# A hybrid attention and DeltaNet block: two operands of a block solve turned by VectorE's 32x32 transposes instead of trips through DRAM

## The chip, the cores and the metric

The kernel runs on one core of a Trainium2 chip. The metric is the device time of one execution in microseconds, lower is better. Engines are named as in the profile: PE (TensorE) multiplies matrices, DVE (VectorE) and ACT (ScalarE) work elementwise, POOL (GpSimd) here sets constants and issues transfers, SP (SyncE) only issues transfers. Each engine takes its instructions in the order in which they stand in its own stream.

## The reference, cut to what matters

One decoder block on 1024 tokens of width 1024: an RMS norm, one wide input projection, two mixers, their gates, an output projection, a residual, a final norm. Mixer A is a dilated window attention. Mixer B, where the change lies, is a gated DeltaNet in chunks of 64 tokens: for each of 8 heads and 16 chunks a unit lower triangular 64x64 matrix must be inverted.

```
k_beta = kc * bc[..., None]
a = jnp.einsum('bhnid,bhnjd->bhnij', k_beta, kc) * decay_strict
t_inv = lax.linalg.triangular_solve(eye + a, jnp.broadcast_to(eye, a.shape),
                                    left_side=True, lower=True, unit_diagonal=True)
u = t_inv @ (vc * bc[..., None])
w = t_inv @ (k_beta * jnp.exp(G)[..., None])
```

All arithmetic is in float32 as far as the output can tell; the kernel splits operands of the large products in two float16 parts and adds three products.

## The kernel before, in words

**Order of the work.** TensorE's order is written out by hand: `Feed` hands out steps of the large projections (three 128x512 products with 512 columns each, about 0.65 us a step), and the small mixers' products are put between them by `feed.tick(n)`. For the other engines a scheduler sets the order when the kernel is built, from priorities and its own idea of times. What stands in an engine's stream is then taken strictly in that order.

**The inverse.** The 8 heads are handled in two halves, `hb` 0 and 1, 64 matrices each. A matrix is cut in 32x32 blocks. `keys_side` (line 1275) makes from the keys the two scalars of each row, `brk` (beta over the key's norm) and `rk` (one over the norm), packs them in `pack`, lets TensorE form the products of keys (`pairs`), multiplies by the decays and leaves the result, transposed, in `MT[hb]`. The diagonal blocks go to DRAM (`m_d`) and come back in `As` with one 32x32 block in each partition. The scalars take the same way: transposed by TensorE (line 1294), copied by ACT (line 1296), stored to `sc_d`, loaded as `bsc` with a block in each partition.

`solve` (line 1305) multiplies `As` by the two scalars (two products on DVE), and in 31 steps of two DVE instructions each (`stmp<-As,X`, then `X<-X,stmp`) builds the inverse of all 128 diagonal blocks in `X`. It scales `X` and writes minus its transpose to `T1`, **which takes the buffer of `As`**: the pool has one buffer with that tag. `X` and `T1` are stored to `u_d` and `t_d`. Four loads bring the blocks of `X` back into `MT[hb]` (called `U` there), two loads bring `T1p`, the operand of the merge, in a layout with a block row in each partition. `T1p` shares the tag and the one buffer with `kd`, a product of the keys that `spill_keys` (line 1214) stores.

The whole solve is recorded with a lowered priority, so the scheduler puts its steps between other DVE work.

`merge` (line 1339) makes the block below the diagonal. `left(g)`: 32 small products of `T1p` and `U` into a bank `ps_S` (L1350), which DVE evicts as `Y`, scaled by `brk` from `pack`. `right(g)`: 32 products of `Y` and `U` into `ps_G` (L1365), copied into `U` by ACT. In TensorE's order stand `left(0)`, five feed steps, `left(1)` interleaved with `right(0)`, five feed steps, `right(1)`. `state_parts` (line 1384) then multiplies `U` by values (`rvt`, L1413) and keys (`kbt`, L1417), evicted as `uw`.

**What runs around it.** While the solves run on DVE, TensorE projects units of the DeltaNet (`gdn`) and gates. Each half of a `gdn` unit (24 products, one of three `ps_mm` banks) is copied by ACT into `xc` and `ca` (two buffers each); DVE adds three shifted products (`ca`, line 83, three in a chain); ACT applies SiLU. The second values unit, projected from 637 to 659 us, is transposed on TensorE by four groups of L1440 into `ps_O`, a tag with **one** bank, evicted by DVE as `rv`. For every unit of weights ACT writes `whi` and DVE `wlo`, two halves each. The queue of SP holds nearly all of these loads and stores, in order: a transfer that waits holds up those behind it.

Of the kernel before, what the change touches and what calls it, by code (L numbers as in the profile page):

```python
# [10 lines left out]
F32 = mybir.dt.float32  # L11
# [3 lines left out]
ALU = mybir.AluOpType  # L15
# [62 lines left out]
def hybrid_block(ctx: ExitStack, tc: tile.TileContext, A):  # L78
    nc = tc.nc
    V, SC, PE, GP = nc.vector, nc.scalar, nc.tensor, nc.gpsimd  # L80
# [4 lines left out]
    def TT(out, in0, in1, op, eng=None):  # L85
        (eng or V).tensor_tensor(out, in0, in1, op)  # L86
# [5 lines left out]
    def bank(tag, bufs):  # L92
        return ps.tile([128, 512], F32, name=f"ps_{tag}", tag=tag, bufs=bufs)
# [26 lines left out]
    def part(n):  # L120
        off[0] += n
        return cons[:, off[0] - n:off[0]]

    ident = part(128)
# [371 lines left out]
    with tc.manual_schedule(engines={nc.vector.engine, nc.scalar.engine}):  # L496
        wq, wk = w_first
        q, k = qk
# [63 lines left out]
        q = [bank("mm", 3), bank("O", 1)]  # L562
# [580 lines left out]
    p2_ = pctx.enter_context(tc.tile_pool(name="gpre2", bufs=1))  # L1143
# [25 lines left out]
    def rnorm(dst, ssum, post):  # L1169

        SC.activation(ssum, ssum, AF.Sqrt, bias=epsc)
        V.reciprocal(dst, ssum)
        if post != 1.0:
            V.tensor_scalar(dst, dst, post, None, op0=ALU.mult)

    def heads_h2(x):
        return x.rearrange("p t (q e) -> p t e q", e=2)
# [34 lines left out]
    def spill_keys(hb):  # L1212

        hs = slice(4 * hb, 4 * hb + 4)
        for g in range(2):
            ts = slice(4 * g, 4 * g + 4)
            k = key_rows(hb, g)
            kd = p2_.tile([128, 4, 4, 64], F32, name="kd", tag="T1p", bufs=1)
            TT(kd, k, bc(eGl[:, ts, hs], 64), ALU.mult)
            nc.sync.dma_start(out=kd_d[ts, :, hs].rearrange("t p h c -> p t h c"), in_=kd)  # L1220
            TT(k, k, bc(bgk[:, ts, hs], 64), ALU.mult)
            nc.sync.dma_start(out=kb_d[hb][:, ts], in_=k)

    def sumsq(hb, src, dst, take=None):

        for t0 in range(0, 8, 2):
            p = bank("S", 2)
            for t in (0, 1):
                for c in range(2):
                    o = (2 * t + c) * 128  # L1230
                    PE.transpose(p[:, o:o + 128],
                                 src[2 * hb + c][:, 2 * (t0 + t):2 * (t0 + t) + 2].rearrange("p c i -> p (c i)"), ident)
            if take:
                take(hb, t0, p)
            with tc.high_priority():
                SC.activation(p, p, AF.Square)
                V.tensor_reduce(dst[:, t0:t0 + 2], p.rearrange("p (t h c) -> p t h c", t=2, c=64), AX.X, ALU.add)
            feed.tick(2)
# [36 lines left out]
    def keys_side(hb):  # L1275
        hsl = slice(4 * hb, 4 * hb + 4)
        sumsq(hb, kT, kss, keep_keys)
        rnorm(rk[:, :, hsl], kss, 1.0)
        TT(brk[:, :, hsl], rk[:, :, hsl], beta[:, :, hsl], ALU.mult)
        TT(bgk[:, :, hsl], brk[:, :, hsl], eG[:, :, hsl], ALU.mult)  # L1280
        pack = p2_.tile([128, 2, 8, 4], F32, name="pack", tag="pack", bufs=2)
        packs.append(pack[:, 0].rearrange("p t h -> p (t h)"))
        for i, x in enumerate((brk, rk)):
            V.tensor_copy(pack[:, i].rearrange("p t (e q) -> p t e q", e=2), heads_h2(x[:, :, hsl]))
        pairs(hb, kT, MT[hb])
        spill_keys(hb)
        m_d = tc.dram_tile([4, 32, 32, 32], F32, name=f"m_d{hb}")
        for kb in range(4):
            b = kb % 2
            nc.sync.dma_start(out=m_d[kb].rearrange("n j i -> j n i"),  # L1290
                              in_=MT[hb][32 * kb:32 * kb + 32].rearrange("p t e q i -> p (t e q) i")[:, :, 32 * b:32 * b + 32])
        feed.tick(4)
        pp = bank("G", 2)
        PE.transpose(pp[0:64, 0:128], pack.rearrange("p a t h -> p (a t h)"), ident)
        packT = p2_.tile([64, 128], F32, name="packT", tag="packT", bufs=1)
        SC.copy(packT, pp[0:64, 0:128])
        sc_d = tc.dram_tile([2, 4, 32, 32], F32, name=f"sc_d{hb}")
        for i in range(2):
            nc.sync.dma_start(out=sc_d[i].rearrange("k n i -> n k i"),
                              in_=packT[32 * i:32 * i + 32].rearrange("p (k i) -> p k i", i=32))  # L1300
        bsc = p2_.tile([128, 2, 32], F32, name="bsc", tag="bsc", bufs=2)
        nc.sync.dma_start(out=bsc, in_=sc_d.rearrange("a k n i -> (k n) a i"))
        return m_d, bsc

    def solve(hb, m_d, bsc):

        As = p2_.tile([128, 32, 32], F32, name="As", tag="As", bufs=1)
        nc.sync.dma_start(out=As.rearrange("p j i -> p (j i)"), in_=m_d.rearrange("k n j i -> (k n) (j i)"))
        TT(As, As, bsc[:, 0, None, :].to_broadcast([128, 32, 32]), ALU.mult)
        TT(As, As, bsc[:, 1, :, None].to_broadcast([128, 32, 32]), ALU.mult)  # L1310
        X = p2_.tile([128, 32, 32], F32, name="X", tag="X", bufs=1)
        GP.memset(X, 0.0)
        GP.memset(X.rearrange("p a b -> p (a b)")[:, ::33], 1.0)
        for k in range(31):
            n = 31 - k
            tmp = p2_.tile([128, 256], F32, name="stmp", tag="stmp", bufs=1)
            tv = tmp[:, :(k + 1) * n].rearrange("p (a b) -> p a b", b=n)
            TT(tv, As[:, k:k + 1, k + 1:].to_broadcast([128, k + 1, n]),
               X[:, :k + 1, k:k + 1].to_broadcast([128, k + 1, n]), ALU.mult)
            TT(X[:, :k + 1, k + 1:], X[:, :k + 1, k + 1:], tv, ALU.subtract)  # L1320
        TT(X, X, bsc[:, 1, None, :].to_broadcast([128, 32, 32]), ALU.mult)
        T1 = p2_.tile([128, 32, 32], F32, name="T1", tag="As", bufs=1)
        V.tensor_scalar(T1, X.rearrange("p j i -> p i j"), -1.0, None, op0=ALU.mult)
        u_d = tc.dram_tile([4, 32, 32, 32], F32, name=f"u_d{hb}")
        t_d = tc.dram_tile([4, 32, 32, 32], F32, name=f"t_d{hb}")
        nc.sync.dma_start(out=u_d.rearrange("k n j i -> (k n) (j i)"), in_=X.rearrange("p j i -> p (j i)"))
        nc.sync.dma_start(out=t_d.rearrange("k n j i -> (k n) (j i)"), in_=T1.rearrange("p j i -> p (j i)"))
        U = MT[hb]
        T1p = p2_.tile([128, 8, 4, 32], F32, name="T1p", tag="T1p", bufs=1)
        for kb in range(4):  # L1330
            b = kb % 2
            if b == 0:
                nc.sync.dma_start(out=T1p[32 * kb:32 * kb + 32].rearrange("p t h j -> p (t h) j"),
                                  in_=t_d[kb].rearrange("n i j -> i n j"))
            nc.sync.dma_start(out=U[32 * kb:32 * kb + 32].rearrange("p t e q i -> p (t e q) i")[:, :, 32 * b:32 * b + 32],
                              in_=u_d[kb].rearrange("n j i -> j n i"))
        return T1p
# [118 lines left out]
    for hb in range(2):  # L1456
        conv_unit(hb, 0, lambda c, hb=hb: qT[2 * hb + c],
                  lambda c, q, hb=hb: nc.scalar.dma_start(out=q_d[2 * hb + c], in_=q))
    gate_unit(5, gate_spill)
    side, solved, packs = [], [], []  # L1460
    for hb in range(2):
        decay(hb)
        side.append(keys_side(hb))
        with tc.high_priority(offset=-SOLVE_LATER):
            solved.append(solve(hb, *side[hb]))
# [206 lines left out]
    for t in range(8):  # L1672
# [21 lines left out]
        for c2 in range(2):  # L1694
            ch = 2 * t + c2
            ov = ob[:, t, 4 * c2:4 * c2 + 4]
            if ch:

                pwq = [bank("S", 2), bank("S", 2)]
                for i in range(2):  # L1700
                    for q in range(2):
                        for e, hb in ((0, 0), (1, 1), (0, 1), (1, 0)):
                            b, c, o = c2 ^ hb, 2 * hb + q, (2 * i + q) * 64
# [44 lines left out]
    for h0 in (0, 2):  # L1748
        for hf in range(2):
# [6 lines left out]
            for hb in range(2):  # L1756
# [8 lines left out]
                n = osp["b", ct]  # L1765
# [19 lines left out]
    for n in range(7):  # L1785
        wo7[n] = []
        for i, l in enumerate("hl"):
            if n == 5:
                t = [late[0].tile([128, 512], F32, name=f"wo5{l}{b}", tag=("gst", "oa")[i], bufs=2).bitcast(F16)
                     .rearrange("p (k n) -> p k n", n=512) for b in range(2)]  # L1790
                wo7[n].append(lambda k, t=t: t[k // 2][:, k % 2])
                continue
            if n == 6:
                t = late[1].tile([128, 2, S], F16, name=f"wo6{l}", tag="oTb", bufs=6)
                t = t.rearrange("p a b -> p (a b)").rearrange("p (k n) -> p k n", n=512)
            else:
                t = fp2.tile([128, 4, 512], F16, name=f"wo{n}{l}")
# [6 lines left out]
                            bufs=1 if n < 4 else 6).rearrange("p l (k i) -> p l k i", i=256) for n in range(7)])  # L1804
# [33 lines left out]
    for pair in range(4):  # L1838
        hf, ps_ = pair // 2, slice(pair % 2 * 128, pair % 2 * 128 + 128)
        rows_ = [Tokens(2 * pair + i) for i in range(2)]  # L1840
        x, q, y = [bank(*b) for b in ((("G", 2), ("G", 2), ("mm", 3)), (("mm", 3),) * 3)[pair % 2]]
# [160 lines left out]
```

## Time and profile before

| | |
|---|---|
| Runs, us | 1072.23, 1076.85, 1076.34; median 1076.34 |
| Profiled execution, us | 1075.46 |
| Its span, first to last instruction, us | 1073.7 |
| Granted TensorE clock, mean | 0.997 |
| Busy in the span: PE, DVE, ACT | 1048.7, 864.4, 559.6 us |
| First solve on DVE | 604.87 to 645.8 us |
| Second solve on DVE | 670.38 to 712.5 us |
| First merge on TensorE, from its first product to the start of `right(1)` | 666.68 to 676.59 us |
| Second merge, the same | 730.27 to 743.30 us |

How to read it: a row of the timeline has the start and the length in us, the engine, the line (a helper's line where a helper records the instruction: L86 is every `tensor_tensor` and L83 every `scalar_tensor_tensor`), the operation, the tile written and the tiles read, shapes, and a count where rows are merged. In square brackets stands the idle time of the engine before the row and what ended it. A row of stretches has for each engine the busy time in the stretch, the granted clock (1.00 is full speed), the busy share of the DMA engines and GB/s. Matmuls overlap: 128x512 products last 0.38 us each and start 0.216 us apart at full clock.

### The profile page before, as it was taken

What the parts mean: (1) busy time and instruction counts of PE and PEld (TensorE: products, weight loads), DVE (VectorE), ACT (ScalarE), POOL (GpSimd) and SP (SyncE); (2) the same over time, 40 slices, a digit from 0 to 9 for tenths busy, and PEclk for the clock granted to TensorE, in tenths of its full rate; (3) what the DMA queues carried; (4) which work ended last, traced back from release to release, by engine and by line L of the source; (5) the groups of instructions that cost most, each with busy time, mean ns of one, the idle gap of its engine ahead of it and who ended that gap; (6) DMA issues with size and microseconds to landing.
All of it is one profiled execution on the core that took longest, in us unless ns stands there. A gap on an engine that the chain in (4) does not pass through costs nothing.

```text
span 1073.7 us, 23669 instructions
## 1 busy us (share of the span) xinstructions
PE 1048.7 (98%) x9398; PEld 639.1 (60%) x9398; DVE 864.4 (81%) x1982; ACT 559.6 (52%) x1272; POOL 56.1 (5%) x107
## 2 busy tenths in 40 slices
PE   7999999999999999999999999999999999999997
PEld 5995585775956855765645544555545555444443
DVE  6897997869878788979966897986588778899834
ACT  6455766566666656547645623244454345443522
POOL 0000000000000000000000000111200000000000
PEclk9999999999999999999999999999999999999999
DMA  8144531632615432641234357785685433763132
GB/s 278 61 131 106 140 105 50 173 95 80 191 67 149 109 105 61 178 120 50 76 123 159 91 130 196 245 242 158 200 267 166 147 98 121 274 225 109 61 117 79
DMA packets 99488, 148.47 MB, mean 138 GB/s; under 512 B 31136, under 2 KB 64416, under 8 KB 98224
## 3 DMA queue, kind: packets, MB, share of 16 engines
q1 hardware_dynamic: 68976, 84.60, 27.4%
q0 software_dynamic: 12320, 44.11, 13.2%
q10 hardware_dynamic: 18080, 18.23, 4.9%
q8 instruction: 74, 1.21, 0.5%
q14 instruction: 38, 0.31, 0.1%
HBM read 91.13 MB, written 36.90 MB: 119 GB/s over the span
## 4 chain that ended last, share of the span: by engine, by line
PE 61%; DVE 27%; ACT 5%; issue 3%; DMA 2%; SPq 1%; ACTq 0%; DVEq 0%
PE ps_mm L183 15%; PE ps_mm L184 14%; PE ps_mm L185 14%; DVE ca L83 4%; DVE wlo L83 2%; DVE X L86 2%; DVE stmp L86 2%; DVE sm L799 2%; PE ps_S L184 2%; PE ps_S L185 2%; PE ps_S L183 2%; DVE tl L86 1%; PE ps_G L813 1%; DVE rt L86 1%; ACT sm L803 1%
## 5 line engine op out<-in xcount | busy, mean ns | idle before, releaser
L185 PE MATMUL ps_mm<-h_hi,wlo 128*128 128x512 f16 (+1 forms) x552 | 208.3, 377 | 0.0
L183 PE MATMUL ps_mm<-h_hi,whi 128*128 128x512 f16 (+1 forms) x492 | 185.6, 377 | 0.0
L184 PE MATMUL ps_mm<-h_lo,whi 128*128 128x512 f16 (+1 forms) x492 | 185.5, 377 | 0.0
L185 PEld LDWEIGHTS <-wlo 128*128 128x128 f16 x788 | 77.2, 98 | 86.5 <-issue 0.6
L183 PEld LDWEIGHTS <-whi 128*128 128x128 f16 x848 | 83.3, 98 | 69.2 <-issue 0.9
L184 PEld LDWEIGHTS <-whi 128*128 128x128 f16 x848 | 83.2, 98 | 68.0 <-issue 1.2
L183 PE MATMUL ps_mm<-whi,h_hi 128*128 128x256 f16 x384 | 105.1, 274 | 0.0
L185 PE MATMUL ps_mm<-whi,h_lo 128*128 128x256 f16 x384 | 104.7, 273 | 0.0
L184 PE MATMUL ps_mm<-wlo,h_hi 128*128 128x256 f16 x384 | 104.7, 273 | 0.0
L803 ACT ACTIVATE sm<-sm,osb 128x128 f32<-128x128 f32 (+1 forms) x160 | 69.5, 435 | 65.0 <-DVE osb L799 60.5
L86 DVE TENSOR_TENSOR tl<-ps_G,th 128x256 f16<-128x256 f32 (+1 forms) x96 | 52.0, 542 | 21.9 <-ACT th L818 21.4
L83 DVE SCALAR_TENSOR_TENSOR wlo<-wstage,whi 128x1024 f16<-128x1024 f32 x50 | 61.0, 1220 | 3.4 <-ACT whi L166 3.2
L799 DVE CUSTOM_DVE_ANT_0 sm<-ps_S,amask 128x128 f32<-128x128 f32 (+1 forms) x192 | 59.4, 348 | 5.2 <-PE ps_S L792 5.2
L83 DVE SCALAR_TENSOR_TENSOR ca<-xc,cw,ca 128x512 f32<-128x512 f32 x72 | 53.9, 748 | 5.3 <-ACT ca L1010 4.6
L166 ACT ACTIVATE whi<-wstage 128x1024 f16<-128x1024 f32 x49 | 51.4, 1051 | 1.7 <-ACT gst L948 0.8
L83 DVE SCALAR_TENSOR_TENSOR whi<-wstage,whi 128x512 f16<-128x512 f32 x60 | 40.9, 689 | 13.6 <-ACT whi L330 13.0
L813 PE MATMUL ps_G<-cons,sm 128*128 128x128 f32 x280 | 47.9, 275 | 3.1 <-ACT sm L803 1.3
L813 PEld LDWEIGHTS ps_G<-cons,sm 128*128 128x128 f32 x280 | 35.5, 141 | 19.3 <-ACT sm L803 4.9
L184 PEld LDWEIGHTS <-h_hi 128*128 128x128 f16 x384 | 45.8, 119 | 1.6
L330 ACT ACTIVATE whi<-wstage 128x512 f16<-128x512 f32 x60 | 37.1, 627 | 18.4 <-DVE wstage L329 13.3
L183 PE MATMUL ps_mm<-h_hi,wlo 128*128 128x512 f16 x120 | 45.6, 380 | 1.0 <-DVE rx L83 1.0
L183 PEld LDWEIGHTS <-h_hi 128*128 128x128 f16 x384 | 45.6, 119 | 1.5
(445 smaller groups left out, 2593.3 us busy)
## 6 DMA issues: line engine op xcount, KB each, us to landing
wstage<-in_w POOLq DMA_DIRECT2D x68, 512.0 KB, 4.6
og<-osb ACTq DMA_DIRECT2D x32, 132.0 KB, 2.1
og<-og SPq DMA_DIRECT2D x32, 132.0 KB, 2.2
gspb<-gst ACTq DMA_DIRECT2D x16, 256.0 KB, 2.5
sga<-gspa SPq DMA_DIRECT2D x8, 512.0 KB, 6.4
wstage<-in_w_up POOLq DMA_DIRECT2D x8, 512.0 KB, 4.7
wos<-in_w_out SPq DMA_DIRECT2D x8, 512.0 KB, 5.3
sgb<-gspb SPq DMA_DIRECT2D x8, 512.0 KB, 5.1
```

Of the source, the lines that this page charges most:

```text
L83: (eng or V).scalar_tensor_tensor(out, in0, scalar, in1, op0=op0, op1=op1)
L86: (eng or V).tensor_tensor(out, in0, in1, op)
L166: in_turn(SC.activation(hi[:, 4 * c:4 * c + 4], st, AF.Copy, scale=W_SCALE))
L183: PE.matmul(out, lhsT=wh(k), rhs=mh(k), start=first and i == 0, stop=False, skip_group_check=True)
L184: PE.matmul(out, lhsT=wh(k), rhs=ml(k), start=False, stop=False, skip_group_check=True)
L185: last_pe[0] = PE.matmul(out, lhsT=wl(k), rhs=mh(k), start=False, stop=last and i == len(ks) - 1, skip_group_check=True).ins.name
L330: in_turn(SC.activation(t[:, b, 0], self.part[name], AF.Copy, scale=W_SCALE))
L799: V.tensor_tensor_reduce(P[:, u, :128 * nk], psc[:, u * 256:u * 256 + 128 * nk], mask, -cexp, -NEG, ALU.add, ALU.min, accum_out=osb[:, 256 ...
L803: SC.activation(P[:, u, :128 * nk], P[:, u, :128 * nk], AF.Exp, bias=osb[:, 256 + hd:257 + hd], scale=-1.0, accum_out=osb[:, 260 + hd:261 ...
L813: PE.transpose(pt[:, c:c + 128], P[:, u, i * 128:i * 128 + 128], ident)
```

## The change

Four edits, all in `keys_side` and `solve`.

1. `pack` is filled by multiplications, `brk` times -1 and `rk` times 1, instead of copies, and `bsc` is made from `pack` by one VectorE transpose in 32x32 blocks. The transpose on TensorE, the copy on ACT, `sc_d` and its four stores and two loads (both halves) go.
2. As the scalar now has the minus sign, the solve adds where it subtracted.
3. `T1p` is written from `X` by one VectorE transpose in 32x32 blocks, straight into the merge's layout. `T1`, `t_d`, its store and the two loads of `T1p` in each half go. So nothing takes `As`'s buffer at the end of a solve any more. The merge's sign sits in `brk`, by which `Y` is scaled.
4. The four loads of `U` come in the order 1, 3, 0, 2.

```diff
         for i, x in enumerate((brk, rk)):
-            V.tensor_copy(pack[:, i].rearrange("p t (e q) -> p t e q", e=2), heads_h2(x[:, :, hsl]))
+            V.tensor_scalar(pack[:, i].rearrange("p t (e q) -> p t e q", e=2), heads_h2(x[:, :, hsl]),
+                            (-1.0, 1.0)[i], None, op0=ALU.mult)
+        bsc = p2_.tile([128, 2, 32], F32, name="bsc", tag="bsc", bufs=2)
+        V.transpose(bsc.rearrange("p a i -> p (a i)"), pack.rearrange("p a t h -> p (a t h)"))
...
-        pp = bank("G", 2)
-        PE.transpose(pp[0:64, 0:128], pack.rearrange("p a t h -> p (a t h)"), ident)
-        packT = p2_.tile([64, 128], F32, name="packT", tag="packT", bufs=1)
-        SC.copy(packT, pp[0:64, 0:128])
-        sc_d = tc.dram_tile([2, 4, 32, 32], F32, name=f"sc_d{hb}")
-        for i in range(2):
-            nc.sync.dma_start(out=sc_d[i].rearrange("k n i -> n k i"),
-                              in_=packT[32 * i:32 * i + 32].rearrange("p (k i) -> p k i", i=32))
-        bsc = p2_.tile([128, 2, 32], F32, name="bsc", tag="bsc", bufs=2)
-        nc.sync.dma_start(out=bsc, in_=sc_d.rearrange("a k n i -> (k n) a i"))
...
-            TT(X[:, :k + 1, k + 1:], X[:, :k + 1, k + 1:], tv, ALU.subtract)
+            TT(X[:, :k + 1, k + 1:], X[:, :k + 1, k + 1:], tv, ALU.add)
         TT(X, X, bsc[:, 1, None, :].to_broadcast([128, 32, 32]), ALU.mult)
-        T1 = p2_.tile([128, 32, 32], F32, name="T1", tag="As", bufs=1)
-        V.tensor_scalar(T1, X.rearrange("p j i -> p i j"), -1.0, None, op0=ALU.mult)
+        T1p = p2_.tile([128, 8, 4, 32], F32, name="T1p", tag="T1p", bufs=1)
+        V.transpose(T1p.rearrange("p t h j -> p j (t h)"), X)
...
-        t_d = tc.dram_tile([4, 32, 32, 32], F32, name=f"t_d{hb}")
...
-        nc.sync.dma_start(out=t_d.rearrange("k n j i -> (k n) (j i)"), in_=T1.rearrange("p j i -> p (j i)"))
...
-        T1p = p2_.tile([128, 8, 4, 32], F32, name="T1p", tag="T1p", bufs=1)
-        for kb in range(4):
+        for kb in (1, 3, 0, 2):
...
-            if b == 0:
-                nc.sync.dma_start(out=T1p[32 * kb:32 * kb + 32].rearrange("p t h j -> p (t h) j"),
-                                  in_=t_d[kb].rearrange("n i j -> i n j"))
```

The change also moves instructions that it doesn't touch, since the scheduler orders anew. TensorE's order is the same but for the two transposes. Rows below are of the two built programs; the lines of the changed kernel are its own, 13 lower behind the edits.

SP, from the last stores ahead of the end of the first solve. Before, the second load of `As` stands behind all traffic of the first solve's result:

```order
L1326 DMA u_d_8342<-X 128x1024
L1327 DMA t_d_8343<-T_8340 128x1024
L1335 DMA MT_7877<-u_d_8342 32x32x32
L1333 DMA T1p<-t_d_8343 32x32x32
L1335 DMA MT_7877<-u_d_8342 32x32x32
L1333 DMA T1p<-t_d_8343 32x32x32
L1335 DMA MT_7877<-u_d_8342 32x32x32
L1446 DMA rv_d<-rv 128x4x128
L1335 DMA MT_7877<-u_d_8342 32x32x32
L1446 DMA rv_d<-rv 128x4x128
L1392 DMA rvt<-rv_d 128x4x256
L1308 DMA As<-m_d_8711 128x1024
```

SP in the changed kernel, the same place:

```order
L1433 DMA rv_d<-rv 128x4x128 x2
L1301 DMA As<-m_d_8701 128x1024
L1318 DMA u_d_8335<-X 128x1024
L1322 DMA MT_7877<-u_d_8335 32x32x32 x4
L1433 DMA rv_d<-rv 128x4x128
L1379 DMA rvt<-rv_d 128x4x256
```

The load of `As` for the second half stands ahead of the store of the first half's `X`, and the four loads of `U` stand together.

DVE behind the first solve, before (the first row is the scaling of `X` that ends it):

```order
L86 TENSOR_TENSOR X<-X,bsc 128x1024
L1323 TENSOR_SCALAR T_8340<-X 128x1024
L83 SCALAR_TENSOR_TENSOR wlo<-wstage,whi 128x1024
L1007 COPY xc<-xc 128x3
L83 SCALAR_TENSOR_TENSOR ca<-xc,cw,ca 128x512 x3
L1005 MEMSET xc 128x3
```

DVE in the changed kernel, from the same row:

```order
L86 TENSOR_TENSOR X<-X,bsc 128x1024
L1316 STREAM_TRANSPOSE T1p<-X 128x32x32
L86 TENSOR_TENSOR As<-As,bsc 128x1024
L83 SCALAR_TENSOR_TENSOR wlo<-wstage,whi 128x1024
L1007 COPY xc<-xc 128x3
L83 SCALAR_TENSOR_TENSOR ca<-xc,cw,ca 128x512
L86 TENSOR_TENSOR As<-As,bsc 128x1024
L83 SCALAR_TENSOR_TENSOR ca<-xc,cw,ca 128x512
L86 TENSOR_TENSOR stmp<-As,X 128x31
L83 SCALAR_TENSOR_TENSOR ca<-xc,cw,ca 128x512
```

The second solve's first product and its steps now stand right behind the first solve and between the conv chains of the second values unit; `wlo` and `ca` stand behind a row that needs the load of `As`.

DVE up to the first `Y` of the first merge, before:

```order
L86 TENSOR_TENSOR rv<-ps_O,bg 128x512
L83 SCALAR_TENSOR_TENSOR ca<-xc,cw,ca 128x512 x3
L86 TENSOR_TENSOR rv<-ps_O,bg 128x512
L83 SCALAR_TENSOR_TENSOR wlo<-wstage,whi 128x1024
L86 TENSOR_TENSOR Y<-ps_S,pack 32x512 x2
```

DVE in the changed kernel, the rows up to the same `Y`:

```order
L86 TENSOR_TENSOR stmp<-As,X 128x256
L83 SCALAR_TENSOR_TENSOR wlo<-wstage,whi 128x1024
L86 TENSOR_TENSOR X<-X,stmp 128x16x16
L86 TENSOR_TENSOR stmp<-As,X 128x255
L86 TENSOR_TENSOR X<-X,stmp 128x17x15
L86 TENSOR_TENSOR stmp<-As,X 128x252
L86 TENSOR_TENSOR Y<-ps_S,pack 32x512 x2
```

Before, no step of the second solve stands ahead of this `Y`; now 17 of its 31 steps and the first half of the 18th do.

## The prediction, put on record before the run

> **What bounds the kernel now.** First the page, then busy time by stretches, then who waited for whom on TensorE from 580 to 780 us, where all of the changed work lies.
>
> ```profile
> PE 1048.7 (98%) x9398; PEld 639.1 (60%) x9398; DVE 864.4 (81%) x1982; ACT 559.6 (52%) x1272; POOL 56.1 (5%) x107
> 600.00:720.00 120.00, 120.00 (x1236) 62.41 (x1234) 106.33 (x222) 45.19 (x76) 10.84 (x19) 1.00 0.62 179
> 720.00:745.00 25.00, 23.57 (x402) 12.67 (x401) 18.05 (x28) 12.51 (x24) 2.17 (x4) 0.93 0.76 202
> PE ps_G L1365 <- DVE Y L86: 1.4, 2, 1.0
> ```
>
> TensorE (second number of a stretch) is busy for all of 600 to 720, VectorE (fourth) for 89% of it. TensorE's order is written out by hand, so time comes off only where it waits, and each wait for VectorE is added in full. Here it waits once, at the second merge, for the eviction Y:
>
> ```profile
> 736.38 0.21 PE L1365 MATMUL ps_G<-MT,Y 32*32 32x32 f32 x1 [0.95 <-DVE Y L86]
> 737.11 0.21 PE L1365 MATMUL ps_G<-MT,Y 32*32 32x32 f32 x1 [0.48 <-DVE Y L86]
> 738.88 0.63 PE L185 MATMUL ps_mm<-h_hi,wlo 128*128 128x512 f16 x1
> ```
>
> The rows in brackets are the wait; with the starts that stretch around it about 1.9 us. Then projection matmuls last 0.63 us instead of 0.38, and the granted clock of the stretch is 0.93. A loss of 0.07 x 25 = 1.75 us, say 1.7: one window at half clock. This merge's wait costs 3.6 in all.
>
> **What the change removes.** Two transposes of pack on TensorE, two ACT copies, twelve DMAs on SP:
>
> ```profile
> L1294 PE MATMUL ps_G<-cons,pack x2: 272/272/273, 590.8 to 623.3; 128*64 128x128 f32 x2
> 643.78 0.22 DVE L86 TENSOR_TENSOR X<-X,stmp 128x60 f32<-128x60 f32 x1
> ```
>
> TensorE saves at most 0.54 us, ahead of waits that VectorE will set, so I count nothing. The new 128x64 transposes of pack aren't in the trace; between nothing and twice the 0.22 of the nearest row, I take 0.15 each. TensorE's waits name none of the loads that go, so their going is worth nothing by itself. The two copies into pack become multiplications of the same size; subtract to add is free; the order of the U loads changes nothing, since all four now go out right behind the store.
>
> **What it moves** is the point. T1 lived in As's buffer; without it, the second solve's As load waits only for the last read of As in the first solve, and both SP and VectorE now have it there (the orders above). VectorE takes its rows in order, so I follow them.
>
> ```profile
> 604.87 1.22 DVE L86 TENSOR_TENSOR As<-As,bsc 128x1024 f32<-128x1024 f32 x1
> 644.04 0.21 DVE L86 TENSOR_TENSOR stmp<-As,X 128x31 f32<-128x31 f32 x1
> 644.53 1.23 DVE L86 TENSOR_TENSOR X<-X,bsc 128x1024 f32<-128x1024 f32 x1
> 645.79 1.05 DVE L1323 TENSOR_SCALAR T<-X 128x1024 f32<-128x1024 f32 x1
> 646.76 1.22 DVE L83 SCALAR_TENSOR_TENSOR wlo<-wstage,whi 128x1024 f16<-128x1024 f32 x1
> 664.43 0.55 SPq L1308 DMA_DIRECT2D As<-m_d  x1
> 670.38 1.23 DVE L86 TENSOR_TENSOR As<-As,bsc 128x1024 f32<-128x1024 f32 x1 [0.31 <-issue]
> DMA to landing us min/median/max: 4.1/5.0/5.9
> ```
>
> The first solve (604.87 to 645.8) keeps its place: VectorE is full there, so 0.15 later at most. T1p's transpose of 128x1024 isn't in the trace: from 0.97 (T's row to the next) to 2.5 (twice the dearest 1024-wide row); I take 1.1, by T's row, and at 2.5 it still ends before As lands. The As load leaves at 644.4, ahead of the store of U on SP, which wants to leave at 645.9 and isn't held up. The last row gives the landing of the two As loads; the second took 5.9 (664.43 to 670.38), so the first 4.1. I take 4.6: As is there at 649.0, and VectorE stands idle from 647.1 with wlo and the conv chains queued behind. Bounds: 647.1 (no wait) and 650.4. On POOL the diagonal of X is set behind a weight load that waits for this wlo, about 652; the first step wants X near 654.
>
> From there to the first Y stand, in the new order, twelve conv steps ca, three wlo and two As products, two rv, and the second solve's first 17 and a half steps. Prices:
>
> ```profile
> 667.93 1.41 DVE L86 TENSOR_TENSOR Y<-ps_S,pack 32x512 f32<-32x512 f32 x2 [2.14 <-PE ps_S L1350]
> 669.37 0.69 DVE L86 TENSOR_TENSOR rv<-ps_O,bg 128x512 f32<-128x512 f32 x1
> 671.52 1.22 DVE L83 SCALAR_TENSOR_TENSOR wlo<-wstage,whi 128x1024 f16<-128x1024 f32 x1
> 672.65 1.22 DVE L86 TENSOR_TENSOR As<-As,bsc 128x1024 f32<-128x1024 f32 x1
> 683.13 0.31 DVE L86 TENSOR_TENSOR stmp<-As,X 128x156 f32<-128x156 f32 x1
> 691.51 0.42 DVE L86 TENSOR_TENSOR stmp<-As,X 128x256 f32<-128x256 f32 x1
> 699.50 0.74 DVE L83 SCALAR_TENSOR_TENSOR ca<-xc,cw,ca 128x512 f32<-128x512 f32 x1
> 700.16 0.38 DVE L86 TENSOR_TENSOR X<-X,stmp 128x220 f32<-128x220 f32 x1
> ```
>
> Start to start: ca 0.66, wlo and As 1.14, rv 0.6. Ten solve steps take 8.4 when alone (683.13 to 691.51); the five before them are shorter, down from those, together about 2.8, the two and a half behind them 2.3; where other work stands between their halves 0.1 is saved, about 14 times, which leaves 12.1. Sum: 7.9 + 5.7 + 1.2 + 12.1 + 0.2 for small copies = 27.1. Y runs from 676.1 to 677.6 (now: 667.93 to 669.3). The second Y follows after rv, wlo and three and a half steps, 4.7, and takes 1.4: 683.7.
>
> Who waits:
>
> ```profile
> 661.62 0.27 PE L1440 MATMUL ps_O<-cons,vT 128*128 128x128 f32 x1
> 671.60 0.21 PE L1365 MATMUL ps_G<-MT,Y 32*32 32x32 f32 x1
> 676.59 0.22 PE L1365 MATMUL ps_G<-MT,Y 32*32 32x32 f32 x2
> 684.47 0.27 PE L1417 MATMUL ps_S<-MT,kbt 64*64 64x64 f32 x4
> 678.83 0.39 SPq L1393 DMA_DIRECT2D kbt<-kb_d  x1
> DMA to landing us min/median/max: 5.6/6.2/6.4
> ```
>
> The transposes at 661.62 write ps_O, which has one bank; its first rv now stands behind nine ca (5.9), four 1024-wide rows (4.6) and eight and a half steps (4.6): with its own 0.6 and the copies 15.9 after As, done at 665.1, so TensorE waits 3.5. The first right() then wants Y at 671.60 + 3.5 = 675.1 and gets it at 677.65: 2.6 more. The second right() comes 5.0 later, at 682.7, and waits to 683.75: 1.0. Last, kbt's load stands behind kd and kb_d on SP, which follow the second Y on VectorE: 3.2 later, 686.9, and it lands 5.9 later at 692.8, where L1417 wants it at 691.6: 1.2. Sum 8.3; L1417 starts at 692.8, not 684.47.
>
> The first of these waits may bring a half-clock window; up to 2.6 of its cost vanish in the next wait, so I add nothing.
>
> **What it gives back.** The second merge's Y is late because ScalarE's evictions lag behind TensorE:
>
> ```profile
> 691.86 0.68 DVE L1424 COPY uw<-ps_G 128x512 f32<-128x512 f32 x1
> 708.80 0.68 DVE L1424 COPY uw<-ps_G 128x512 f32<-128x512 f32 x1
> 703.82 0.38 PE L185 MATMUL ps_mm<-h_hi,wlo 128*128 128x512 f16 x1
> 712.13 0.59 ACT L1008 COPY xc<-ps_mm 128x512 f32<-128x512 f32 x1
> 727.38 0.38 PE L185 MATMUL ps_mm<-h_hi,wlo 128*128 128x512 f16 x1
> 732.07 0.59 ACT L1008 COPY xc<-ps_mm 128x512 f32<-128x512 f32 x1
> 735.64 0.68 DVE L86 TENSOR_TENSOR Y<-ps_S,pack 32x512 f32<-32x512 f32 x1
> ```
>
> The half that ended at 704.2 was taken at 712.13, 7.9 later, that of 727.76 at 732.07, 4.3 later, and Y stands behind that half's ca. The lag comes from uw rows placed amid the second solve. Now that solve ends first: after the second Y four key products (4.6), rv (0.6), the last ten steps (6.4), X and T1p (2.4), so uw at 697.7. TensorE is 8.3 late by then: 689.4 on the old clock, 2.5 earlier than 691.86. Between 703.82 and 727.38 TensorE ends four halves, 5.9 each; ScalarE and VectorE's round took 5.0 (712.13 to 732.07, four). The second pair of uw stands behind two rounds and no solve steps, near 703.5 instead of 708.80, so the lag of 7.9 falls to about 3 and shrinks by 0.9 a half: gone by 727.8. Then Y could run at 731.5 and is wanted at 735.2. The 3.6 go.
>
> **Sum:** +8.3 - 3.6 = +4.7. The profiled execution took 1075.46 (span 1073.7), 0.9 below the median 1076.34. So 1080.2 beside 1075.46, and 1081.0 beside the median.
>
> **A rule weighed.** In the trace waits of 0.95 and 0.48 us among 32x32 matmuls were followed by the half clock. [...] The trace shows the window right behind them and no other cause, and I go by it.
>
> **Rivals.**
> - *The second merge still waits.* For it: the local order around that Y is the same as before. Against: the lag that sets it shrinks. Then +8.3: 1084.6; with one more window at half clock that no wait hides, 1086.3.
> - *The half clock isn't the wait's doing.* Then removing that wait gives 1.9, not 3.6: +6.4, 1082.7. Against: the first merge has the same small matmuls and no wait, and its stretch is granted 1.00. [...]
> - *Other side: the solve's steps only fill VectorE's idle time.* For it: there is some, 2.14 at the first Y now. If Y were ready in time, only the 3.6 would remain: 1072.7. It decides at the second Y, which must end by 676.6; by my rows it ends 34.7 after As lands, so As would have to land by 642, before the first solve is over. Against it: nearly everything.
>
> **Chances:** forecast 0.61, second merge waits 0.22, clock 0.10, other side 0.07. The forecast's own range: As at 647.1 and kbt landing in 5.6 give 2.3 less, 1078.6; As at 650.4 gives 1.4 more, 1082.4. The range reaches from 1078.6 less the 4.1 by which the lowest run lies under the median, 1074.5, to 1086.3 plus the 0.5 of the highest, 1086.8. About 0.5% (5.4 us) is what a measurement of this kernel can tell from no change, so 1081.7 divides: slower 0.22 + 0.10 + a quarter of the forecast, 0.48; faster 0.02; the rest, 0.50, is the same.
>
> **What would show it.** Right: the second As product at about 649 to 651; L1440 waiting for rv near 661; first right() near 678 waiting for Y; L1365 near 743 with no wait, and the granted clock 1.00 there. Wrong: Y before 672 on VectorE, no wait between 655 and 695, or a wait at the second merge as now.

## The result and the profile after

| | before | changed |
|---|---|---|
| Runs, median (lowest to highest), us | 1076.84 (1072.23 to 1078.00), 6 runs | 1085.01 (1083.56 to 1088.52), 6 runs |
| Ratio to before, 95% interval | | 1.0093, 1.0076 to 1.0110 |
| Profiled execution; its span, us | 1075.46; 1073.7 | 1086.79; 1085.0 |

The changed kernel is slower by 0.9%, some 8 to 12 us by the interval (the medians are 8.2 apart). The forecast was 4.7. All lines of the changed kernel are 13 lower than before (L1365 is L1352, L1417 is L1404, L1424 is L1411).

The same two stretches as before, of the changed kernel (second number TensorE, fourth VectorE, then ScalarE; behind POOL the granted clock, the DMA share and GB/s):

```profile
600.00:720.00 120.00, 112.71 (x1130) 58.34 (x1129) 101.94 (x214) 41.49 (x68) 10.17 (x19) 0.99 0.57 167
720.00:745.00 25.00, 23.02 (x285) 11.84 (x283) 14.27 (x23) 10.49 (x19) 2.62 (x5) 1.00 0.42 130
```

TensorE, full from 600 to 720 before, is now idle there for 7.3 us. VectorE, named by most of the forecast's waits, is busy for 4.4 us less than before: it waits too. Whom TensorE waited for from 580 to 780 us, in the changed kernel (total, times, longest; two more rows have 0.4 and 0.2 us):

```profile
PE ps_G L1352 <- DVE Y L86: 3.8, 4, 1.5
PE ps_mm L183 <- ACT ca L1010: 2.0, 1, 2.0
PE ps_S L1404 <- ACT uw L1411: 1.9, 1, 1.9
PE ps_O L1427 <- DVE rv L86: 1.6, 1, 1.6
PE ps_S L1404 <- DMA kbt<-kb_d: 1.4, 1, 1.4
```

Rows four and five and half of row one were forecast, for the first merge. The other half of row one is the wait of the second merge, which was to go. Rows two and three name ScalarE; no step of the forecast had them. In the order of time, on TensorE:

```profile
663.48 0.63 PE L1427 MATMUL ps_O<-cons,vT 128*128 128x128 f32 x4 [1.65 <-DVE rv L86]
675.22 0.21 PE L1352 MATMUL ps_G<-MT,Y 32*32 32x32 f32 x1 [1.49 <-DVE Y L86]
675.94 0.21 PE L1352 MATMUL ps_G<-MT,Y 32*32 32x32 f32 x1 [0.48 <-DVE Y L86]
682.43 0.76 PE L1352 MATMUL ps_G<-MT,Y 32*32 32x32 f32 x36
691.85 0.34 PE L1404 MATMUL ps_S<-MT,kbt 64*64 64x64 f32 x8 [1.36 <-DMA kbt<-kb_d]
707.90 0.28 PE L1404 MATMUL ps_S<-MT,kbt 64*64 64x64 f32 x3 [1.94 <-ACT uw L1411]
726.20 0.38 PE L183 MATMUL ps_mm<-h_hi,whi 128*128 128x512 f16 x1 [1.98 <-ACT ca L1010]
742.08 1.20 PE L1337 MATMUL ps_S<-T1p,MT 32*32 32x32 f32 x64
748.97 0.21 PE L1352 MATMUL ps_G<-MT,Y 32*32 32x32 f32 x1 [1.32 <-DVE Y L86]
749.70 0.21 PE L1352 MATMUL ps_G<-MT,Y 32*32 32x32 f32 x1 [0.48 <-DVE Y L86]
```

Read this against the rows of before: the first kbt product starts at 691.85 instead of 684.47, 7.4 later (forecast 8.3). By the second merge the delay is larger, not smaller: two more waits, 1.94 and 1.98, stand on the way, left(0) starts 11.8 later (742.08, before 730.27), and the wait for Y behind it is still there; right(1) starts 10.9 later (754.21, before 743.30), since the half-clock window of before is gone. Why, shows on ScalarE of the changed kernel:

```profile
695.25 0.59 ACT L1411 COPY uw<-ps_S 128x512 f32<-128x512 f32 x1 [2.58 <-DMA rv_d<-rv]
695.87 0.41 ACTq L1413 DMA_DIRECT2D wn_d<-uw  x1
707.26 0.59 ACT L1411 COPY uw<-ps_S 128x512 f32<-128x512 f32 x1 [11.43 <-DMA wn_d<-uw]
708.30 1.06 ACT L166 ACTIVATE whi<-wstage 128x1024 f16<-128x1024 f32 x1 [0.45 <-ACT uw L1411]
718.42 0.59 ACT L1411 COPY uw<-ps_S 128x512 f32<-128x512 f32 x1 [0.74 <-ACT qT L1021]
723.95 0.59 ACT L1411 COPY uw<-ps_S 128x512 f32<-128x512 f32 x1 [4.95 <-DMA wn_d<-uw]
```

and of the kernel before:

```profile
694.72 0.59 ACT L1424 COPY uw<-ps_S 128x512 f32<-128x512 f32 x1 [4.53 <-DMA wn_d<-uw]
711.64 0.59 ACT L1424 COPY uw<-ps_S 128x512 f32<-128x512 f32 x1 [3.20 <-DMA wn_d<-uw]
```

Each group of `state_parts` evicts four `uw` tiles, two on each engine, and `uw`, `Y` and `rv` share three buffers. In the first group ScalarE's first `uw` comes first (695.25) and VectorE's two follow (696.81), so ScalarE's second, the fourth, takes the buffer of its first and waits until that one's store has landed. Before, that took 4.5 and 3.2 us; now 11.4 and 5.0, and all that ScalarE has behind it (`whi`, `xc`, `ca`) stands still, with it VectorE, which waits 11.3 us for that `whi`. The store left at 695.87. What SP issued around it, in the changed kernel:

```profile
693.48 0.32 SPq L1380 DMA_DIRECT2D kbt<-kb_d  x1
695.03 0.32 SPq L1318 DMA_DIRECT2D u_d<-X  x1
695.46 0.38 SPq L1379 DMA_DIRECT2D rvt<-rv_d  x1
695.92 3.51 SPq L1380 DMA_DIRECT2D kbt<-kb_d  x2
699.49 7.79 SPq L1322 DMA_DIRECT2D MT<-u_d  x4
```

The second solve's scaling of X ends near 695 now, before at 712.5. Its end frees the buffers of `As` and `X` for the second half's kbt, and sends the store of X and the four loads of U. All that, and the first half's own second rvt and kbt, leaves between 693.5 and 707.3. The stretch 690 to 700 before and, below it, changed:

```profile
690.00:700.00 10.00, 10.00 (x166) 5.41 (x164) 9.49 (x22) 3.84 (x6) 2.75 (x5) 1.00 0.59 161
```
```profile
690.00:700.00 10.00, 8.64 (x158) 4.91 (x158) 7.59 (x17) 1.18 (x2) 2.23 (x4) 1.00 0.98 329
```

The DMA engines go from 0.59 busy to 0.98. ScalarE's store takes 11.3 us to land beside SP's traffic, although its own queue holds only the end of one more store (issued at 692.71, landed 3.6 later). From 690 to 707 the packets of SP's queue take 79% of the engines' time and those of ScalarE's 11%. Before, SP's took 27% there, and the two stores of `uw` that ScalarE issued at 690.22 and 695.33 landed in 4.4 and 3.8 us.

### The profile page after: what moved, and what is told of

Same layout as the page of the kernel before. It is cut to its first block, busy times and chain, and to the rows that moved or that the text cites. A ratio compares the mean times of both kernels' runs of the same rounds, so it can differ in the third digit from the quotient of the medians.

```text
span 1085.0 us, 23649 instructions
## 1 busy us (share of the span) xinstructions
PE 1050.1 (97%) x9396; PEld 639.2 (59%) x9396; DVE 865.2 (80%) x1984; ACT 559.3 (52%) x1270; POOL 56.4 (5%) x107
## 4 chain that ended last, share of the span: by engine, by line
PE 65%; DVE 23%; DMA 4%; ACT 4%; issue 3%; SPq 1%; ACTq 0%; DVEq 0%
PE ps_mm L183 16%; PE ps_mm L185 15%; PE ps_mm L184 15%; DVE ca L83 4%; DVE wlo L83 2%; DMA wn_d<-uw 2%; PE ps_G L813 2%; DVE X L86 2%; PE ps_S L185 2%; PE ps_S L183 2%; PE ps_S L184 2%; DVE stmp L86 2%; DVE sm L799 1%; SPq L629 1%; DVE tl L86 1%
```

## The experiments

Two theories first. **A**: the loss is the place of the second solve; it delays the first merge on VectorE, and its early end crowds the stores of `uw`, for whose buffer ScalarE waits. **B**: the transposes and the new order of the loads cost the time themselves. The ratio is to the kernel before on the same chip (medians there 1075.21, 1076.61 and 1076.52 for the three groups). It is not the quotient of the two medians, which differs from it by up to 0.2%.

| run | median, us | ratio, 95% interval |
|---|---|---|
| early solve alone | 1086.73 | 1.0101, 1.0084 to 1.0118 |
| late solve, with the change | 1077.45 | 1.0016, 1.0004 to 1.0028 |
| As load behind the loads of U | 1083.19 | 1.0070, 1.0054 to 1.0085 |
| loads of U later | 1084.02 | 1.0084, 1.0063 to 1.0104 |
| loads of U and kbt later | 1082.81 | 1.0064, 1.0043 to 1.0085 |
| change, fourth buffer | 1078.06 | 1.0017, 1.0007 to 1.0026 |
| As load behind the loads of U, fourth buffer | 1075.12 | 0.9994, 0.9983 to 1.0005 |
| late solve, fourth buffer | 1075.21 | 0.9997, 0.9987 to 1.0008 |
| before, fourth buffer | 1074.21 | 0.9988, 0.9976 to 1.0000 |
| before, eight feed steps | 1074.67 | 1.0002, 0.9986 to 1.0018 |
| As load behind, fourth buffer, eight steps | 1075.29 | 0.9999, 0.9987 to 1.0010 |
| before, fourth buffer, eight steps | 1074.69 | 0.9988, 0.9978 to 0.9998 |

### The early solve without the change

The kernel before, with one tag altered:

```diff
-        T1 = p2_.tile([128, 32, 32], F32, name="T1", tag="As", bufs=1)
+        T1 = p2_.tile([128, 32, 32], F32, name="T1", tag="T1p", bufs=1)
```

> The kernel before, without any transpose on VectorE and without the new order of the loads: only T1 is put in the buffer of T1p instead of that of As, so that the load of As for the second solve may leave early. Theory A: the loss is there, 1082 to 1087, with the first Y on VectorE near 675 and a wait of ScalarE for the buffer of uw of about 10 us. Theory B: 1074 to 1078.

Measured 1.0101: all of the loss, with no transpose on VectorE, all loads through DRAM and the old order of the loads. Its VectorE and ScalarE:

```profile
674.27 1.41 DVE L86 TENSOR_TENSOR Y<-ps_S,pack 32x512 f32<-32x512 f32 x2
```
```profile
702.22 0.58 ACT L1424 COPY uw<-ps_S 128x512 f32<-128x512 f32 x1 [6.97 <-DMA wn_d<-uw]
723.84 0.58 ACT L1424 COPY uw<-ps_S 128x512 f32<-128x512 f32 x1 [9.88 <-DMA wn_d<-uw]
```

The first Y and the waits for the buffer, 16.9 us together, are about those of the changed kernel (16.4). B falls: what acts is the buffer that `As` no longer shares. The way from there to TensorE is in part another: it waits 0.99 us for `rvt`, 1.57 for `kbt` and 0.81 for `ca`, none for `uw`, and the granted clock is 0.79 from 704 to 712. So the crowded transfers can also hold TensorE directly.

### The change with a late solve

```diff
-        with tc.high_priority(offset=-SOLVE_LATER):
-            solved.append(solve(hb, *side[hb]))
+        if hb == 0:
+            with tc.high_priority(offset=-SOLVE_LATER):
+                solved.append(solve(hb, *side[hb]))
...
+        if hb == 0:   # in merge, behind left(0)
+            T1 = p2_.tile([128, 32, 32], F32, name="T1", tag="As", bufs=1)
+            V.tensor_copy(T1[32:64, 0], Ys[0][32:64, 0])
+            with tc.high_priority(offset=-SOLVE_LATER):
+                solved.append(solve(1, *side[1]))
```

> Everything of the change is kept, but the load of As for the second solve is held until the first Y: a small tile in As's buffer is written from Y, and the second solve follows it, so VectorE has it about where it stood before the change. Theory A (the loss is the place of the second solve on VectorE, which makes the first merge wait 7.4 us, and its end, which sends its loads of U into the stretch where uw is stored): both go, 1073 to 1077. Theory B (the transposes on VectorE and the new order of the loads of U cost the time themselves): 1082 or more, as the changed kernel.

Measured 1.0016, 1077.45 us: 0.45 above A's upper end, far from B. TensorE waits for nothing at the first merge; ScalarE waits for the buffer about as little as before (9.3 us in all, before 7.7); the second Y is late as before. The interval leaves 0.3% at most for what the transposes, the new order of the loads and the hold cost together.

### The load of As behind the loads of U

```diff
+        T1 = p2_.tile([128, 32, 32], F32, name="T1", tag="As", bufs=1)
+        V.tensor_copy(T1[:, 0], X[:, 0])
+        t_d = tc.dram_tile([128, 32], F32, name=f"t_d{hb}")
...
+        nc.sync.dma_start(out=t_d, in_=T1[:, 0])   # behind the store of X
```

> The change, with the load of As for the second solve held until the first T1p is written and 16 KB of a small tile in As's buffer are stored behind it, so that SP has it behind the four loads of U, near 653 instead of 644. Two As products, one group of steps and no waiting wlo stand ahead of the first Y. Theory A: the waits of the first merge shrink to 0 to 3 us, the rest follows, 1074 to 1080. Theory B: 1082 or more.

Measured 1.0070: a miss, and the most useful one. The first merge's waits did go, to 0.72 for kbt and 0.48 at the second merge, as A said; and the time stayed. One wait took their place, on TensorE, and its cause on ScalarE:

```profile
723.29 0.59 PE L183 MATMUL ps_mm<-h_hi,whi 128*128 128x512 f16 x1 [8.15 <-ACT ca L1010]
```
```profile
721.57 0.58 ACT L1415 COPY uw<-ps_S 128x512 f32<-128x512 f32 x1 [11.48 <-DMA wn_d<-uw]
722.06 0.59 ACT L1008 COPY xc<-ps_mm 128x512 f32<-128x512 f32 x1
722.53 0.70 ACT L1010 ACTIVATE ca<-ps_mm,cw 128x512 f32<-128x512 f32 x1
```

X is scaled by 703 here, so the loads of U now meet the stores of the second pair of `uw`. `ca`, which TensorE waits for, stands right behind the `uw` that waits. Around that wait the granted clock is 0.58 (720 to 728), which adds to the loss. The two halves of A are separate costs: this kernel has only the second.

### Fewer transfers beside the store

The change, with the loads of U (first run), and of the second half's kbt too (second run), held until VectorE's second pair of `uw`:

```diff
+                    if not hb and g == 1 and x == 0 and r == 1:
+                        for kb in range(4):   # one column of what the loads overwrite
+                            rr = slice(32 * kb, 32 * kb + 32)
+                            V.tensor_copy(MT[1][rr].rearrange("p t e q i -> p (t e q) i")[:, 0, 32 * (kb % 2):32 * (kb % 2) + 1],
+                                          uw[rr, 0, 0, 0:1])
+                        held[0]()             # the four loads of U
```

The second run has ahead of `held[0]()` also

```diff
+                        for a in ("As", "X"):   # the buffers of the second half's kbt
+                            hold = p2_.tile([128, 32, 32], F32, name="hold" + a, tag=a, bufs=1)
+                            V.tensor_copy(hold[:, 0, 0:1], uw[:, 0, 0, 0:1])
```

> The change, with the four loads of U of the second solve held until the second pair of uw on VectorE (near 717 instead of 699). Theory A1 (these loads, in many small packets, keep the stores of uw from landing; ScalarE waits 11.4 us for the buffer, and that sets the waits of 1.9 us for uw near 708 and 2.0 us for ca near 726): the store lands in 4 to 6 us, both waits go, and the second merge's wait of 1.9 us may go too, 1079 to 1083. Theory A2 (the loads of kbt and rvt alone fill the queues): the store still takes 9 to 11 us and the time is that of the changed kernel, 1084 to 1086.

> The change, three buffers, with the four loads of U and the two kbt loads of the second half held until the second pair of uw on VectorE. Theory A: the stores of uw land in 3 to 5 us as in the kernel before, ScalarE's waits fall to 3 to 5 us each, no wait for uw or ca on TensorE, 1078 to 1081, a little below the run in which only the loads of U were held (1084, 1081 to 1087). If other traffic (rvt, the stores themselves) fills the queues: 1083 to 1086.

Measured 1.0084 and 1.0064, both above what A said, and not clearly below the changed kernel in the first case. In the profiled executions the waits do shrink (first run, ScalarE):

```profile
700.66 0.59 ACT L1419 COPY uw<-ps_S 128x512 f32<-128x512 f32 x1 [5.98 <-DMA wn_d<-uw]
718.35 0.59 ACT L1419 COPY uw<-ps_S 128x512 f32<-128x512 f32 x1 [5.95 <-DMA wn_d<-uw]
```

and TensorE waits for `ca` only 0.3 us, in the second run 0.5. But that first profile was of the fastest of six runs (1080.76; the others 1082.49 to 1087.22), so it may show the better end only. In the second run, with the kbt loads gone too, ScalarE's waits are 5.9 and 6.6, still above the 4.5 and 3.2 of before. So these loads are a part of the crowd and not all of it. What share the first half's own rvt and kbt have wasn't tried and stays open.

### A fourth buffer

The transfers as they are, only the buffer free: `gm`, used before 640 us, moves into the shared tag, which pays for the room.

```diff
-                gm = p2_.tile([128, 256], F32, name="gm", tag="gm", bufs=2)
+                gm = p2_.tile([128, 256], F32, name="gm", tag="rv", bufs=4)
...
-                    uw = p2_.tile([128, 4, 2, 64], F32, name="uw", tag="rv", bufs=3)
+                    uw = p2_.tile([128, 4, 2, 64], F32, name="uw", tag="rv", bufs=4)
```

(Y and rv likewise.) The order of TensorE, SP and POOL is the changed kernel's; VectorE's differs in rows of `gm` alone, ScalarE's in the place of the store's issue behind its second `uw`.

> The change, with four buffers instead of three for uw, Y and rv; the room comes from gm, which shares them (it is used only before 640 us). The order of VectorE and SP stays word for word, so the transfers stay as they are; only ScalarE's fourth uw needs no store to land. Theory A (that wait of 11.4 us and the 5.0 us one of the second pair hold ScalarE's queue, and with it the conv chain up to the second Y): the waits of 1.9 us near 708 and 2.0 us near 726 go, ScalarE's last uw stands near 713, the second Y follows 24 us later, near 738, before it is wanted, so that its 1.9 us go too; 1078 to 1081. Theory C (the crowded queues also bring kbt and rvt late, so TensorE waits for them instead): 1083 to 1086.

Measured 1.0017. The stores of `uw` still take 5.4 to 7.5 us to land, yet ScalarE's second `uw` waits 1.17 instead of 11.43, and TensorE's list for 580 to 800 us is down to the first merge:

```profile
694.04 0.59 ACT L1411 COPY uw<-ps_S 128x512 f32<-128x512 f32 x1 [1.17 <-DMA rv_d<-rv]
```
```profile
PE ps_G L1352 <- DVE Y L86: 2.0, 2, 1.5
PE ps_O L1427 <- DVE rv L86: 1.6, 1, 1.6
PE ps_S L1404 <- DMA kbt<-kb_d: 0.4, 1, 0.4
```

VectorE and TensorE at the second merge:

```profile
690.25 0.34 PE L1404 MATMUL ps_S<-MT,kbt 64*64 64x64 f32 x8 [0.42 <-DMA kbt<-kb_d]
736.08 1.20 PE L1337 MATMUL ps_S<-T1p,MT 32*32 32x32 f32 x64
745.55 0.34 PE L1352 MATMUL ps_G<-MT,Y 32*32 32x32 f32 x9
```
```profile
737.33 1.41 DVE L86 TENSOR_TENSOR Y<-ps_S,pack 32x512 f32<-32x512 f32 x2 [0.20 <-PE ps_S L1337]
```

The kbt product is 5.8 later than before (690.25 to 684.47), right(1) of the second merge only 2.25 (745.55 to 743.30), and the profiled execution 2.15 (1077.61 to 1075.46). So the 3.6 are given back here, just as the forecast had them: Y now waits for its own products instead of making TensorE wait. The merge itself shows the same price: from the first product of left(0) to the start of right(1) it takes 9.47 us here (736.08 to 745.55) and 13.03 before. A's two parts are thus shown apart: the first merge's delay, less what it gives back, costs 0.2%, and the buffer the other 0.8%.

### The fourth buffer in the other kernels

> The change with the second As load behind the loads of U (as in the run with the small tile in As's buffer, 1083.2, where TensorE waited 8.2 us for ca) and a fourth buffer for uw. Theory A (those 8.2 us are ScalarE's wait for the buffer of uw): they go, the first merge's waits stay near 1.2 us, the second Y waits 0 to 1.9: 1074 to 1078. If the 8.2 us come from a late VectorE or from TensorE's own order: 1081 to 1084.

Measured 0.9994, as A said: the 8.15 us for `ca` are gone with the buffer alone (from 1.0070), although the DMA engines are as full there from 712 to 724 (shares by four us 1.03, 1.08 and 1.01; without the buffer 1.02, 1.06 and 1.11).

> The change with the second solve held until the first Y (as in the run of the late solve), and the fourth buffer. Theory A: neither the first merge's waits nor the uw waits nor the second Y's wait, 1071 to 1075, at or below the kernel before. If the late solve's 1077 had another cause: 1076 to 1078.

Measured 0.9997, 1075.21, 0.2 above A's upper end: level with before. The second merge's wait for Y, 1.3 and 0.5 us, did not go as A had it.

> The kernel before with the same fourth buffer. Theory A (the second Y comes 24 us behind ScalarE's last uw, which waits 4.5 and 3.2 us for stores before): uw 3 to 8 us earlier, the second merge's wait of 1.9 us goes and with it the window at half clock of 1.7 us, 1071 to 1074. If that wait has another cause (the order around Y alone): 1075 to 1077.

Measured 0.9988, interval up to 1.0000: at most a small gain, and not the mechanism stated. ScalarE's last `uw` ends 3.9 us earlier (708.3 for 712.2), but its next SiLU waits for VectorE:

```profile
715.32 0.63 ACT L1021 ACTIVATE qT<-ca 128x512 f32<-128x512 f32 x1 [5.25 <-DVE ca L83]
```

VectorE has the end of the second solve ahead of that `ca`, until 712.9, and Y comes at 735.05 for 735.64; of these 0.6 us, 0.5 are there at the first Y already (667.45 for 667.93). In the kernel before, buffer and solve hold up the same chain, and either is enough. The wait of 0.86 and 0.48 us stays, with no half-clock window behind it.

### What the second merge's wait is worth

```diff
         for _ in left(0):
             pass
-        feed.tick(MERGE_TICKS)
+        feed.tick((MERGE_TICKS, 8)[hb])
```

> The kernel before with eight feed steps instead of five between left(0) and right(0) of the second merge: it measures what the wait there is worth, which the forecast put at 1.9 us of wait and 1.7 us of half clock. If both go: ratio 0.9967, about 1073. If the half clock is not bound to that wait (it stood behind it in the profile of before, but not behind waits of the same length in four other runs): 0.9982 or a little more, about 1074.7. If the wait moves to right(1): 1.000.

Measured 1.0002, 0.9986 to 1.0018. The 3.6 us (0.9967) are excluded; the wait alone (0.9982) lies just below the interval, though the two medians stand about that far apart. The wait and the half clock are gone in the profile, but three others are new (total, times, longest):

```profile
PE ps_mm L183 <- ACT zs L1488: 1.3, 1, 1.3
PE ps_S L1350 <- DMA T1p<-t_d: 0.9, 1, 0.9
PE ps_G L1365 <- DVE ca L83: 0.7, 1, 0.7
```

The last two stand inside the merge. From the first product of left(0) to right(1) it takes 13.87 us (729.77 to 743.64); less the three added steps of 0.65 that is 11.9, against 13.03 before and 9.47 where nothing waits. So the steps took away only a part of what the merge loses, and this run does not price the whole of it.

> The same, and eight feed steps instead of five (2 us more of projection) between left(0) and right(0) of the second merge, so that its Y has time. Theory A: no wait at the second merge either, 1072 to 1076, below the changed kernel and level with the kernel before or below it. If that wait only moves to right(1): as the run without it.

> The kernel before with the fourth buffer for uw (0.9988 by itself) and with the eight feed steps. If the two add: 0.995 to 0.998, 1071 to 1074, the fastest of all. If the buffer alone had already made Y early enough: 0.9988 as without the steps.

Measured 0.9999 and 0.9988, the same as without the steps. Nothing adds. The nearest to a gain is the kernel before with the fourth buffer, 0.1%, at the edge of what these runs can tell (up to 1.0000, with the steps up to 0.9998). No other kernel of the study is faster than the kernel before.

## Why the prediction was wrong

Point by point, by its own steps, from the profiled executions:

- *T1p's transpose 1.1 us*: 1.95, inside its bounds (0.97 to 2.5). *bsc 0.15*: 0.24.

```profile
645.50 1.95 DVE L1316 STREAM_TRANSPOSE T1p<-X 128x1024 f32<-128x1024 f32 x1
647.40 1.23 DVE L86 TENSOR_TENSOR As<-As,bsc 128x1024 f32<-128x1024 f32 x1
674.48 0.68 DVE L86 TENSOR_TENSOR Y<-ps_S,pack 32x512 f32<-32x512 f32 x1
```

- *As lands at 649.0, VectorE idle before it*: the As product starts at 647.40, right behind the transpose, without a wait. The load landed in 3.4 us. That was the lower bound of the forecast.
- *27.1 us of rows to the first Y*: 647.40 to 674.48, 27.1. Right.
- *The first merge costs 8.3*: 7.4. Of it 1.9 at L1427 (forecast 3.5; As came 1.6 earlier), 2.5 to the first right() (2.6), 1.5 to the second (1.0), 1.5 for kbt (1.2). The third part is a half-clock window and no wait for Y: "added nothing" for such a window was wrong, "1.0" for the wait too, and they all but cancel.
- *uw at 697.7 on VectorE*: 696.81. Near.
- *The second merge's wait costs 3.6*: 13.03 us of merge before, 9.47 without wait and window. Right.

```profile
696.81 1.26 DVE L1411 COPY uw<-ps_G 128x512 f32<-128x512 f32 x2
716.93 1.28 DVE L1411 COPY uw<-ps_G 128x512 f32<-128x512 f32 x2
```

- **The step that failed:** "The second pair of uw stands behind two rounds and no solve steps, near 703.5 instead of 708.80, so the lag of 7.9 falls to about 3". With the 8.3 that is 711.8; it stood at 716.93. The step followed VectorE's `uw` and took ScalarE's for granted. ScalarE's second `uw` needs a buffer, and that needs a store to land; the two rows of before that say so (4.53 and 3.20) were in the trace and were not read. The step also took the landing as given, while the change itself sends SP's transfers into that stretch. In place of -3.6 came +3.9 on TensorE, and the 1.8 us wait for Y stayed; of the 3.6, only the half clock went there. Of the signs of being wrong that the forecast names, one came: a wait at the second merge as before.
- The run with a fourth buffer is the forecast's own mechanism with this step mended: +5.8 and -3.6. The early solve alone does not give the chain back, and (by the kernel before with a fourth buffer) neither does the buffer alone. Nor do the 3.6 come without TensorE's delay. With four buffers the second merge's Y stands at 735.05 in the kernel before, 737.33 in the changed one, 736.57 with the load of As behind the loads of U and 736.88 with the late solve. Only the changed kernel doesn't wait for it, and there TensorE wants it 5.8 us later. So what is given back is a part of the delay, and no run shows it as a gain by itself.
- Two slips in the sums change nothing: 649.0 and 15.9 make 664.9, not 665.1, and 1081.0 less 2.3 is 1078.7, not 1078.6.

The rival "the second merge still waits", 1084.6, has the right number and in part the right place, for another reason: the lag did not shrink. It did not see the two waits for ScalarE, so that its number comes so near is luck. The rival about the clock: the window is gone at the second merge though the wait is there, so wait and window do not go one for one; its sum, 1082.7, is below the measured interval. The other side, 1072.7, is excluded: As would have had to land by 642.

## What to carry to other kernels

A change that frees a buffer is a change of order: look first at what was held back by that buffer and goes early now, with every transfer that goes out at its end. Where an engine evicts into a buffer that a store must free, its whole queue hangs on the landing time of that store (here ScalarE stood for 11.43 us, for a store that took 11.3 to land), so list these waits of before even where they cost nothing, and ask what the change will put beside those stores. One more buffer there can be worth more than the transfers that were saved: here it took the changed kernel from 1.0093 to 1.0017. And a wait that goes because the engine comes later is no gain.

## What the runs showed of the hardware

- The 32x32 transpose of 128x1024 float32 takes 1.95 us on VectorE, written with a stride, where a product of that size takes 1.22 and the multiplication by -1 that read `X` with a stride took 1.05 (L1323 before); 128x64 takes 0.24.
- In these profiles half-clock windows follow TensorE's waits for Y at the merges only sometimes. Behind the first merge's 1.3 to 1.5 and 0.48 us there was one in all five profiles that had that wait (granted clock 0.57 to 0.69 from 676 to 680). Behind the second merge's 1.3 and 0.5 us there was none in the changed kernel, but one in the kernel with the load of As behind and a fourth buffer. The changed kernel's first merge, then that kernel's second:

```profile
676.00:680.00 4.00, 4.00 (x129) 2.30 (x130) 3.86 (x8) 1.15 (x2) 0.53 (x1) 0.57 0.60 192
736.00:744.00 8.00, 6.22 (x141) 3.08 (x141) 6.24 (x9) 4.18 (x9) 0.00 (x0) 0.79 0.03 11
```

What decides it, no run here shows. The length of the wait alone does not: at the second merge, with four buffers, 1.31 and 0.48 us were followed by a window in the kernel with the load of As behind (granted clock 0.88 and 0.69 from 736 to 740 and 740 to 744) and by none in the late solve (1.00 in both). At the changed kernel's first merge TensorE was idle for some 2 us (1.49 and 0.48) ahead of the window.
